# One decoder layer on one core: where the first tokens' block sums are made, how the FFN's buffers are laid out, and when the second tokens' row work is issued

## Chip, core and metric

The kernel runs on one core of a Trainium2 chip, in one launch. The metric is device microseconds of one execution, and less is better. The engines are TensorE (PE, with its weight loads as PEld), VectorE (DVE), ScalarE (ACT), GpSimd (POOL) and SyncE (SP, which here only issues DMAs). Each engine works through a queue of its own, in an order fixed when the program is built. A build-time scheduler makes that order from the program's order, priorities and its own estimate of when each instruction can start; a context `high_priority(offset=n)` moves what is inside it n places ahead (or behind, when negative).

## What is computed

One layer over 2048 tokens of width 1024, all in float32. The attention part (sliding window, state-space and compressed/selected attention) ends in a mixing product, and the FFN follows:

```
x = x + einsum('ble,ed->bld', mixed, w_out)      # mixed: three normed mixer outputs, 1024 wide
h2 = rms_norm(x, norm2_g)
hid = relu(einsum('blf,...', h2, w_up))          # 1024 -> 4096
x = x + einsum('blf,fd->bld', hid * hid, w_down) # 4096 -> 1024
```

## The kernel before

**Products.** A float32 operand is split into a rounded high part and the rest (`split`: a cast on ACT, a subtraction on DVE), and each product is three matmuls. In the FFN each 2 x 2 block product is made of seven products instead of eight, over sums and differences of blocks. The seven are named by digits and always run in the order `ORDER = "1675243"`. Factors 1, 2 and 3 are blocks of the normed tokens themselves; 5, 7, 6 and 4 are differences of blocks.

**Attention's last stage (`phase_mix`).** It goes over 16 tiles of 128 tokens. For tile i `finish_steps` lists: load the mixer rows into the tile `mix` (tag `mix`, one buffer) and the input rows into `box["x"]` (`mx` in the trace, two buffers); turn `mix` (L1190, L1192); 48 matmuls with the 16 tiles of w_out (L77 to L79, "fillers", at low priority); add and square (L1205, L1208); and for i < 8 scale the rows (`next_rows`, L1217), turn them and scale by the gain (`next_turned`, L1225, L1228), and store both halves to `hT` in DRAM (L1229). The list of tile i - 1 is merged into the steps of tile i. Everything in it shares one PSUM bank (`pw`), and the next tile's turn starts when this tile's steps are over.

**FFN up (`phase_up`).** Two groups of 1024 tokens (p = 0, 1), each against 16 slices of w_up (f). A step (p, f) is seven products of 12 matmuls. `first()` makes the first group's seven factors at the start: it loads four blocks of `hT` into the places of factors 4 and 3 (tiles `ft`), makes the four differences with `minus` on DVE and POOL (L1347), splits each into `fh` and `fl`, and loads factors 2 and 3 again through the two buffers `f_x` (`fx`). `weights(0, 0)`, the first slice of w_up (`ur`, sums `fs`, splits `uh`, `ul`), is issued in it ahead of the splits. For the second group, `fetch(m)` loads rows (`fxr`) after every third step, `sums(m)` scales them on ACT (L1380), turns them (L1385, L1387), stores the blocks, makes four differences on POOL (L1392, tile `fxt`) and stores these to `sums` in DRAM; the whole of `sums(m)` is issued at the end of step f = 3m + 2. In the last step of p = 0 the second group's factors are loaded and split one by one (`fetch_factor`, `refill`), each after the product that last used its place.

**FFN down (`phase_down`).** Eight slices of w_down, four token groups each, seven products of 12 matmuls. The split weights `dw` lie in one pool of seven, the 40 accumulators `acc` in two pools.

**Where things lie.** Pools are stacked from a common base, in the order in which they are opened, and a tile waits until what lay in its bytes is done with. Adding up the pool sizes gives, for the end of the attention (kilobytes of each partition, from the base): bias tables up to 22, keys and values `kAs` ... `Vs` 22 to 58, queries and small rows to 73, `th`/`tl`/`oT`/`ot` 73 to 85, four score slabs 85 to 117, `mx` and `mix` 120 to 132, `mh` and `ml` 132 to 140.2, and the 16 tiles of w_out from byte 143,584 on. In `phase_up` before, the seven factors fill 0 to 112, `f_s` 112 to 118, `f_x` 118 to 134, `f_ru` (raw w_up) 134 to 146, `f_st` 146 to 156, `f_u` (split w_up) 156 to 184 and `f_e` 184 to 204.

Of the kernel before, what the change touches and what calls it, by code (L numbers as in the profile page):

```python
# [16 lines left out]
P = 128  # L17
# [934 lines left out]
RING = 6  # L952


def phase_mix(tc, C, x, gains, B, cmp, w_out, out_norm_g, g2, pc, oa_d, ob, x1, hT, rr, rh, ss_a, ss_b, r_d, release):
    nc = tc.nc
    kcA, kcB, vc = cmp
    with ExitStack() as ctx:
# [210 lines left out]
        def finish_steps(i, oc):  # L1169
# [61 lines left out]
            def filler(n, k):  # L1231
                with tc.high_priority(offset=ENDS.get(i, -FILL)):
# [7 lines left out]
            return res + ([next_rows, lambda: next_turned(0), lambda: next_turned(1)] if i < NT // 2 else [])  # L1240

        def front(i):

# [50 lines left out]
AHEAD = 5  # L1294
LAG_SLOT = 2


def split(nc, dh, dl, src):

    nc.scalar.copy(dh, src)  # L1300
    nc.vector.tensor_tensor(dl, src, dh, op=ALU.subtract)  # L1301


def phase_up(tc, C, x1, rr, g2, hT, xs, w_up, vd):
# [7 lines left out]
    with ExitStack() as ctx:  # L1312
        def pool(name, bufs, **kw):
            return ctx.enter_context(tc.tile_pool(name=name, bufs=bufs, reuse_waits="tile", **kw))
        hp = pool("f_h", 1)
        es = pool("f_s", 3)
        xp = pool("f_x", 2)
        ru = pool("f_ru", 6)
        st = pool("f_st", 5)
        up_ = pool("f_u", 7)  # L1320
        ev = pool("f_e", 10)
        g2t = pool("f_g", 1).tile([P, NK], F32, name="f_g2")
        ps_u = pool("f_psu", 2, space=PSUM)
        hh, hl, W = {}, {}, {}

        for o in ORDER:
            for n in "hl":
                hp.tile([P, HALF, 4, P], F32R, tag=n + o, name=f"fo{n}{o}")
        own = {"1": (0, 0), "2": (0, 1), "3": (1, 1)}

        def slot(p, o):
            hh[o], hl[o] = (hp.tile([P, HALF, 4, P], F32R, tag=n + o, name=f"f{n}{p}{o}") for n in "hl")
# [6 lines left out]
        def first():  # L1339

            at = {n: hp.tile([P, HALF, 4, P], F32, tag=tag, name="ft" + n)
                  for n, tag in (("11", "h4"), ("12", "l4"), ("22", "h3"), ("21", "l3"), ("5", "h2"), ("7", "l2"), ("6", "h5"))}
            for n in ("11", "12", "22", "21"):
                nc.sync.dma_start(at[n], hT[0, int(n[1]) - 1, int(n[0]) - 1])

            def minus(eng, dst, x, y):
                eng.tensor_tensor(at[dst], at[x], at[y], op=ALU.subtract)  # L1347

            def keep(o, src):
                slot(0, o)  # L1350
                split(nc, hh[o], hl[o], src)
            W["u"] = weights(0, 0)
            minus(nc.vector, "5", "12", "11")
            minus(nc.gpsimd, "7", "22", "12")
            keep("1", at["11"])
            minus(nc.vector, "6", "22", "5")
            keep("6", at["6"])
            minus(nc.gpsimd, "21", "21", "6")
            keep("7", at["7"])
            keep("5", at["5"])  # L1360
            keep("2", loaded(hT[(0, *own["2"])], "02"))
            keep("4", at["21"])
            keep("3", loaded(hT[(0, *own["3"])], "03"))

        rows = {}

# [5 lines left out]

        def sums(m):

            xr = rows.pop(m)
            x = xp.tile([P, 4, HALF, P], F32, tag="x", name=f"fxb{m}")
            B, T = {}, {}
            for b in range(2):
                r = xr[:, b].rearrange("p k t -> p (k t)")
                nc.scalar.activation(r, r, AF.Copy, scale=rr[:, 8 + 4 * b + m:9 + 4 * b + m])  # L1380
            for n, (b, k) in enumerate(((0, 0), (1, 0), (1, 1), (0, 1))):
                B[b, k] = x[:, n]
                pt = ps_u.tile([P, HALF, P], F32, tag="d", name=f"fpt{m}{n}")
                for j in range(HALF):
                    nc.tensor.transpose(pt[:, j], xr[:, b, HALF * k + j], C["ident"])  # L1385
                for j in range(HALF):
                    nc.scalar.activation(x[:, n, j], pt[:, j], AF.Copy, scale=g2t[:, HALF * k + j:HALF * k + j + 1])  # L1387
                nc.sync.dma_start(hT[1, b, k, :, :, m], x[:, n])
            t = xp.tile([P, 4, HALF, P], F32, tag="x", name=f"fxt{m}")
            for n, (o, x_, y) in enumerate((("5", (1, 0), (0, 0)), ("6", (1, 1), "5"), ("7", (1, 1), (1, 0)), ("4", (0, 1), "6"))):  # L1390
                T[o] = t[:, n]
                nc.gpsimd.tensor_tensor(T[o], B[x_], T[y] if y in T else B[y], op=ALU.subtract)  # L1392
                nc.sync.dma_start(xs[n, :, :, m], T[o])

        def fetch_factor(o):
            rows[o] = loaded(hT[(1, *own[o])] if o in own else xs["5674".index(o)], "1" + o)

        def refill(o):

            slot(1, o)  # L1400
            split(nc, hh[o], hl[o], rows.pop(o))

        def weights(p, f):
# [98 lines left out]

        steps = [(p, f) for p in range(2) for f in range(NF)]
        with tc.high_priority(offset=UP_HOIST):
            first()
            nc.sync.dma_start(g2t, g2[0].rearrange("(k p) -> p k", p=P))
        for n, (p, f) in enumerate(steps):
            last = (p, f) == (0, NF - 1)
            if last:
                for o in ORDER[:2]:  # L1510
                    fetch_factor(o)
            for k, (o, step) in enumerate(zip(ORDER, up(p, f))):
                step()
                if last:
                    refill(o)
                    if k + 2 < 7:
                        fetch_factor(ORDER[k + 2])
            if p == 0 and f % 3 == 0 and f < 12:
                fetch(f // 3)
            if p == 0 and f % 3 == 2 and f < 12:  # L1520
                sums(f // 3)
            if n + 1 < len(steps):
                W["u"] = weights(*steps[n + 1])


def phase_down(tc, x1, w_down, vd, out):
# [4 lines left out]
    FC = 512  # L1531
    NC = DFF // FC
    N = 512
    LOW = 27
    with ExitStack() as ctx:
        def pool(name, bufs, **kw):
            return ctx.enter_context(tc.tile_pool(name=name, bufs=bufs, reuse_waits="tile", **kw))
        wp = pool("d_w", 7)
        ep = pool("d_e", 4)
        a_low = pool("d_a", 1)  # L1540
        rp = pool("d_r", 1)
        vr = pool("d_vr", 3)
        tp = pool("d_t", 3)
        vp = pool("d_v", 6)
        a_high = pool("d_b", 1)
        ps = pool("d_ps", 2, space=PSUM)
# [7 lines left out]

        def start_acc(m):
            for n in ("u", "22", "11", "21", "12"):
                pl = a_low if places.index((m, n)) < LOW else a_high
                acc[m, n] = pl.tile([P, N], F32, tag=f"acc{m}{n}", name=f"acc{m}{n}")
# [12 lines left out]
        def weights(c, res):  # L1571
# [107 lines left out]
def trunk(tc, x, norm1_g, w_in, qk_g, sinks, rel_bias, a_re, a_im, log_dt, b_re, b_im, c_re, c_im, d_skip, glu_w, glu_b,  # L1679
# [3 lines left out]
    with ExitStack() as ctx:  # L1683
# [27 lines left out]
        sums = dr.tile([4, P, HALF, 4, P], F32, name="sums")  # L1711
# [13 lines left out]
        with ExitStack() as c_g:  # L1725
# [18 lines left out]
        phase_mix(tc, C, x, gains, B, cmp, w_out, out_norm_g, norm2_g, pc, oa_d, ob, x1, hT, rr, rh_c, ss_a, ss_b, r_d, c_u.close)  # L1744
# [68 lines left out]
```

## Time and profile before

| | |
|---|---|
| median of 3 runs | 2646.47 us (2642.21 to 2647.43) |
| the profiled execution | 2648.5 us |
| its span, first to last instruction | 2646.7 us |
| PE busy in the span | 2505.8 us, 95% |
| granted TensorE clock, mean | 0.981 of 2.4 GHz |
| attention's last w_out matmul starts | 1354.2 us |
| first FFN product starts / second starts | 1370.3 / 1378.3 us |
| last product of FFN up, first of FFN down | 2024.2 / 2026.1 us |

Times in the text are microseconds from the start of the span. Engines are told by busy time; a matmul's record overlaps the next one's, so what counts on PE is the distance between starts. An idle time is put down to the release that came last.

### The profile page before, as it was taken

What the parts mean: (1) busy time and instruction counts of PE and PEld (TensorE: products, weight loads), DVE (VectorE), ACT (ScalarE), POOL (GpSimd) and SP (SyncE); (2) the same over time, 40 slices, a digit from 0 to 9 for tenths busy, and PEclk for the clock granted to TensorE, in tenths of its full rate; (3) what the DMA queues carried; (4) which work ended last, traced back from release to release, by engine and by line L of the source; (5) the groups of instructions that cost most, each with busy time, mean ns of one, the idle gap of its engine ahead of it and who ended that gap; (6) DMA issues with size and microseconds to landing.
All of it is one profiled execution on the core that took longest, in us unless ns stands there. A gap on an engine that the chain in (4) does not pass through costs nothing. (4 is left out here: it accounts for less than half of the span.)

```text
span 2646.7 us, 39486 instructions
## 1 busy us (share of the span) xinstructions
PE 2505.8 (95%) x13480; PEld 2116.4 (80%) x13480; DVE 1796.4 (68%) x3427; ACT 1315.2 (50%) x2774; POOL 1124.1 (42%) x1193
## 2 busy tenths in 40 slices
PE   8999999899889999999969999999999999999999
PEld 7998989677677777777848777778887888888887
DVE  3835764765686677778666556675555788888886
ACT  5344333765575666656535455544444443344442
POOL 2014442421233332313157666575654344454447
PEclk9999999899899999999989999999999999999999
DMA  4352333522222121101145666665555644444435
GB/s 124 81 149 74 87 77 86 151 63 55 67 87 69 61 65 47 49 27 45 44 158 174 192 191 195 206 202 155 148 151 166 213 131 135 129 127 127 128 96 195
DMA packets 388906, 312.71 MB, mean 118 GB/s; under 512 B 54998, under 2 KB 357724, under 8 KB 387040
## 3 DMA queue, kind: packets, MB, share of 16 engines
q1 hardware_dynamic: 352608, 285.01, 36.2%
q10 hardware_dynamic: 36096, 25.17, 3.0%
q8 instruction: 107, 1.75, 0.3%
q14 instruction: 95, 0.78, 0.1%
HBM read 201.06 MB, written 104.85 MB: 116 GB/s over the span
## 5 line engine op out<-in xcount | busy, mean ns | idle before, releaser
L1300 ACT CAST v<-vr 128x512 fp32r<-128x512 f32 x224 | 139.8, 624 | 307.5 <-DMA vr<-vd 147.0
L1301 DVE TENSOR_TENSOR v<-vr,v 128x512 fp32r<-128x512 f32 x224 | 232.6, 1045 | 81.2 <-ACT v L1300 81.0
L77 PE MATMUL pm<-wh,hh 128*128 128x256 f32 (+2 forms) x768 | 233.9, 305 | 5.4 <-ACT u_st L156 3.6
L78 PE MATMUL pm<-wl,hh 128*128 128x256 f32 (+2 forms) x768 | 226.9, 296 | 2.5 <-DVE wl L137 2.5
L79 PE MATMUL pm<-wh,hl 128*128 128x256 f32 (+2 forms) x768 | 227.0, 296 | 0.0
L1612 PE MATMUL pdc<-dw,v 128*128 128x512 f32 x768 | 185.2, 390 | 2.3 <-DVE acc L1633 1.9
L1612 PE MATMUL pda<-dw,v 128*128 128x512 f32 x768 | 185.0, 390 | 2.4 <-ACT dw L1300 1.4
L1612 PE MATMUL pdb<-dw,v 128*128 128x512 f32 x768 | 184.6, 389 | 0.1
L1612 PEld LDWEIGHTS pda<-dw,v 128*128 128x128 f32 x768 | 144.0, 188 | 33.3 <-ACT dw L1300 2.7
L1612 PEld LDWEIGHTS pdc<-dw,v 128*128 128x128 f32 x768 | 143.9, 188 | 33.3 <-DVE acc L1633 2.8
L1612 PEld LDWEIGHTS pdb<-dw,v 128*128 128x128 f32 x768 | 144.1, 188 | 30.3 <-issue 0.5
L1421 POOL TENSOR_TENSOR fs<-ur,ur 128x512 f32<-128x512 f32 x64 | 92.3, 1443 | 153.9 <-DMA ur<-in_w_up 138.2
L1301 DVE TENSOR_TENSOR ul<-ur,uh 128x512 fp32r<-128x512 f32 x96 | 102.7, 1072 | 78.3 <-ACT uh L1300 75.5
L1300 ACT CAST uh<-fs 128x512 fp32r<-128x512 f32 x128 | 78.6, 622 | 153.0 <-PE pub L1450 60.1
L77 PEld LDWEIGHTS pm<-wh,hh 128*128 128x128 f32 x768 | 147.9, 193 | 8.4 <-ACT u_st L156 3.8
L78 PEld LDWEIGHTS pm<-wl,hh 128*128 128x128 f32 x768 | 147.8, 193 | 6.6 <-DVE wl L137 3.2
L79 PEld LDWEIGHTS pm<-wh,hl 128*128 128x128 f32 x768 | 147.5, 192 | 0.1
L1301 DVE TENSOR_TENSOR ul<-fs,uh 128x512 fp32r<-128x512 f32 x128 | 137.0, 1073 | 13.9 <-ACT uh L1300 13.6
L1450 PE MATMUL pua<-fh,uh 128*128 128x512 f32 x256 | 103.7, 405 | 24.9 <-ACT uh L1300 15.7
L1466 POOL TENSOR_TENSOR ev<-e,e 128x512 f32<-128x512 f32 x64 | 100.8, 1574 | 33.7 <-ACT e L1463 33.7
L77 PE MATMUL pw<-wo_h,mh 128*128 128x512 f32 x256 | 109.3, 427 | 4.4 <-ACT mh L1192 2.8
L845 DVE TENSOR_TENSOR tls<-pps,ths 128x512 fp32r<-128x512 f32 (+1 forms) x144 | 92.7, 657 | 28.5 <-ACT ths L844 21.8
(535 smaller groups left out, 7574.8 us busy)
## 6 DMA issues: line engine op xcount, KB each, us to landing
vr<-vd SPq DMA_DIRECT2D x224, 256.0 KB
ur<-in_w_up SPq DMA_DIRECT2D x128, 256.0 KB
vd<-ev SPq DMA_DIRECT2D x128, 256.0 KB
vd<-e ACTq DMA_DIRECT2D x64, 256.0 KB
dr<-in_w_down SPq DMA_DIRECT2D x32, 512.0 KB
wr<-in_w_in SPq DMA_DIRECT2D x40, 256.0 KB
x<-in_x SPq DMA_DIRECT2D x16, 512.0 KB
mx<-in_x SPq DMA_DIRECT2D x16, 512.0 KB
```

Source lines behind the costliest of these rows:

```text
L77: nc.tensor.matmul(out, sh, mh, start=first, stop=False)
L78: nc.tensor.matmul(out, sh, ml, start=False, stop=False)
L79: nc.tensor.matmul(out, sl, mh, start=False, stop=last)
L845: nc.vector.tensor_tensor(tl[:, 0:nb], pt[:, 0:nb], th[:, 0:nb], op=ALU.subtract)
L1300: nc.scalar.copy(dh, src)
L1301: nc.vector.tensor_tensor(dl, src, dh, op=ALU.subtract)
L1421: nc.gpsimd.tensor_tensor(t, x, y, op=op)
L1450: nc.tensor.matmul(bank[b], w[:, k], h[o][:, k], start=first and k == 0 and n == 0, stop=k == HALF - 1 and n == 2, skip_group_check=True)
L1466: nc.gpsimd.tensor_tensor(tile_("v" + o), x, y, op=op)
L1612: nc.tensor.matmul(bank[b, q], x[:, q, j], y[:, j], start=first and j == 0 and n == 0, stop=j == 1 and n == 2, skip_group_check=True)
```

## The change

- In tiles 4 to 7 of the attention, a new step `partner`, put after three fillers, loads the two stored half rows of tile i - 4 into a tile of tag `mix`; a new last step `next_sums` makes the four differences on POOL and stores them to `xs`, which gets a second copy for the first group. The first half of these tiles is no longer stored to `hT`, as nothing reads it.
- `first()` is gone. All seven factors of the first group come through `f_x` with `fetch_factor` and `refill`, as the second group's do.
- The pools of `phase_up` and `phase_down` get another order. `g2t` is padded to 224 bytes (`PAD`).
- `sums(m)` becomes a list of seven pieces, issued between the products of steps f = 3m + 1 and 3m + 2. The block (1, 0) is no longer stored.

```diff
-                nc.sync.dma_start(hT[0, i // 4, half, :, :, i % 4], hx[:, 4 * half:4 * half + 4])
+                if i < 4 or half:
+                    nc.sync.dma_start(hT[0, i // 4, half, :, :, i % 4], hx[:, 4 * half:4 * half + 4])
+            def partner():
+                old = box["old"] = fp.tile([P, 2, 4, P], F32, tag="mix", name=f"mixs{i}", bufs=1)
+                for half in range(2):
+                    nc.sync.dma_start(old[:, half], hT[0, 0, half, :, :, i - 4])
+            def next_sums():
+                old, hx = box["old"], box["x"].rearrange("p (b k t) -> p b k t", b=2, t=P)
+                for o, dst, a, b in (("5", old[:, 0], hx[:, 0], old[:, 0]), ("7", hx[:, 0], hx[:, 1], hx[:, 0]),
+                                     ("6", hx[:, 1], hx[:, 1], old[:, 0]), ("4", old[:, 1], old[:, 1], hx[:, 1])):
+                    nc.gpsimd.tensor_tensor(dst, a, b, op=ALU.subtract)
+                    nc.sync.dma_start(xs[0, "5674".index(o), :, :, i - 4], dst)
...
+            if NT // 4 <= i < NT // 2:
+                res.insert(6, partner)
+                res.append(next_sums)
...
-        hp = pool("f_h", 1)
-        es = pool("f_s", 3)
-        xp = pool("f_x", 2)
-        ru = pool("f_ru", 6)
-        st = pool("f_st", 5)
-        up_ = pool("f_u", 7)
-        ev = pool("f_e", 10)
-        g2t = pool("f_g", 1).tile([P, NK], F32, name="f_g2")
+        factors(ORDER[:1])
+        st = pool("f_st", 5)
+        xp = pool("f_x", 2)
+        ru = pool("f_ru", 6)
+        up_ = pool("f_u", 7)
+        factors(ORDER[1:3])
+        ev = pool("f_e", 10)
+        es = pool("f_s", 3)
+        g2t = pool("f_g", 1).tile([P, PAD], F32, name="f_g2")
+        factors(ORDER[3:])
...
+            return [lambda b=b: scaled(b) for b in range(2)] + [
+                lambda n=n, b=b, k=k: turned(n, b, k) for n, (b, k) in enumerate(((0, 0), (1, 0), (1, 1), (0, 1)))] + [summed]
...
         with tc.high_priority(offset=UP_HOIST):
-            first()
-            nc.sync.dma_start(g2t, g2[0].rearrange("(k p) -> p k", p=P))
+            for o in ORDER[:2]:
+                fetch_factor(0, o)
+            for k, o in enumerate(ORDER):
+                refill(0, o)
+                if k == 0:
+                    W["u"] = weights(0, 0)
+                if k + 2 < 7:
+                    fetch_factor(0, ORDER[k + 2])
...
+            if p == 0 and f % 3 == 1 and f < 12:
+                parts = dict(zip(((1, 1), (1, 3), (1, 5), (2, 0), (2, 2), (2, 4), (2, 6)), sums(f // 3)))
...
-            if p == 0 and f % 3 == 2 and f < 12:
-                sums(f // 3)
...
-        wp = pool("d_w", 7)
-        ep = pool("d_e", 4)
-        a_low = pool("d_a", 1)
+        w_low = pool("d_w", 2)
+        tp = pool("d_t", 3)
         rp = pool("d_r", 1)
         vr = pool("d_vr", 3)
-        tp = pool("d_t", 3)
         vp = pool("d_v", 6)
-        a_high = pool("d_b", 1)
+        ep = pool("d_e", 4)
+        w_high = pool("d_w2", 5)
+        ap = pool("d_a", 1)
...
+        for m, n in places[-LATE:] + places[:-LATE]:
+            ap.tile([P, N], F32, tag=f"acc{m}{n}", name=f"acc{m}{n}")
...
-                t = wp.tile([P, 2, 2, N], F32R, tag="w", name=f"dw{c}{o}")
+                t = (w_low if o in ORDER[:2] else w_high).tile([P, 2, 2, N], F32R, tag="w", name=f"dw{c}{o}")
```

## Rows read from the trace of the kernel before

**Rows 1.** Stretches: length, engines' busy us (instructions), granted clock, DMA share, GB/s.
```profile
1335.20:1354.60 19.40, 14.93 (x59) 10.79 (x57) 9.53 (x6) 4.25 (x8) 12.55 (x21) 0.91 0.60 244
1354.60:1381.80 27.20, 8.84 (x25) 5.93 (x25) 21.57 (x13) 12.73 (x16) 17.46 (x14) 0.62 0.41 135
1381.80:1640.00 258.20, 249.31 (x1109) 203.76 (x1109) 157.44 (x168) 136.73 (x261) 175.54 (x115) 0.99 0.63 184
1742.00:2000.00 258.00, 258.00 (x1140) 213.70 (x1139) 146.46 (x176) 122.91 (x203) 152.84 (x108) 1.00 0.53 155
1700.00:1742.00 42.00, 31.27 (x111) 23.45 (x110) 29.99 (x25) 22.61 (x29) 22.41 (x12) 0.88 0.77 247
2020.00:2060.00 40.00, 35.72 (x151) 27.29 (x150) 30.11 (x34) 20.45 (x32) 15.25 (x9) 1.00 0.76 249
```

**Rows 2.** The chain that ended last: start, us, twelve matmuls of one product.
```profile
1741.73 2.72 PE pud L1450 x12
```

**Rows 3.** Timeline of PE: start, us, instruction, idle before it and releaser.
```profile
1354.22 0.39 PE L79 MATMUL pw<-wo_h,ml 128*128 128x512 f32 x1
1370.33 0.80 PE L1450 MATMUL pua<-fh,uh 128*128 128x512 f32 x1 [15.72 <-ACT uh L1300]
1378.31 0.50 PE L1450 MATMUL pud<-fh,uh 128*128 128x512 f32 x1 [0.91 <-ACT uh L1300]
```

**Rows 4.** Timeline of SP's queue at the end of the attention.
```profile
1338.45 2.00 SPq L1344 DMA_DIRECT2D ft<-hT  x4
1354.89 2.18 SPq L1409 DMA_DIRECT2D ur<-in_w_up  x4
```

**Rows 5.** Timeline of ACT there.
```profile
1354.43 1.90 ACT L1300 CAST fh<-ft 128x2048 fp32r<-128x2048 f32 x1 [6.83 <-POOL ft L1347]
```

**Rows 6.** Instructions of line 1347 (differences in `first`): ns min/median/max, first, last.
```profile
L1347 POOL TENSOR_TENSOR ft<-ft,ft x2: 4520/5308/6096, 1348.3 to 1359.0; 128x2048 f32<-128x2048 f32 x2
```

**Rows 7.** Timeline of DVE: the last read of the bias table.
```profile
1317.95 0.75 DVE L823 CUSTOM_DVE_ANT_0 slw<-pqw,b_sel,mx 128x512 f32<-128x512 f32 x1 [1.51 <-PE pqw L821]
```

**Rows 8.** Waits of PE, 1385 to 1640: us in total, times, longest.
```profile
PE pua L1450 <- ACT e L1470: 7.4, 3, 2.7
PE fpt L1385 <- ACT fxb L1387: 1.5, 3, 0.7
```

**Rows 9.** Timeline of ACT around 1460.
```profile
1460.75 2.42 ACT L1380 ACTIVATE fxr<-fxr,rr 128x1024 f32<-128x1024 f32 x2 [6.90 <-issue]
```

**Rows 10.** Timeline of SP's queue just ahead of that.
```profile
1450.49 4.32 SPq L1393 DMA_DIRECT2D sums<-fxt  x4
1454.98 1.61 SPq L1371 DMA_DIRECT2D fxr<-x  x2
```

**Rows 11.** Stretches in attention: tiles 4 and 7 without fillers; tiles 8 to 12.
```profile
928.70:939.80 11.10, 8.22 (x62) 7.01 (x61) 7.00 (x17) 7.44 (x21) 4.18 (x11) 1.00 0.20 71
1055.50:1066.80 11.30, 9.49 (x67) 7.99 (x67) 8.49 (x28) 9.01 (x23) 4.93 (x13) 1.00 0.23 83
1066.80:1298.00 231.20, 221.67 (x1398) 184.51 (x1397) 179.50 (x501) 137.59 (x283) 54.08 (x127) 1.00 0.10 34
```

**Rows 12.** Instructions of line 1392, differences on POOL of 128 x 512.
```profile
L1392 POOL TENSOR_TENSOR fxt<-fxb x8: 1288/1515/1745, 1448.0 to 1638.9; 128x512 f32<-128x512 f32 x8
```

**Rows 13.** SP's queue: a load of `mix` in the attention.
```profile
903.99 0.38 SPq L1176 DMA_DIRECT2D mix<-oa_d  x1
```

**Rows 14.** POOL: the last scaling of that `mix`.
```profile
908.97 0.69 POOL L1181 TENSOR_SCALAR mix<-mix,r_b 128x512 f32<-128x512 f32 x1
```

**Rows 15.** ACT: the next tile's turned rows are read.
```profile
939.84 0.59 ACT L1192 CAST mh<-ptx 128x512 fp32r<-128x512 f32 x1
```

**Rows 16.** Instructions on `slw`, 780 to 1090: DVE reads one operand from PSUM.
```profile
L823 DVE CUSTOM_DVE_ANT_0 slw<-pqw,b_sel,mx x31: 731/748/751, 780.4 to 1084.1; 128x512 f32<-128x512 f32 x31
```

**Rows 17.** Instructions on `ul`, 1381 to 1700: DVE reads both operands from SBUF.
```profile
L1301 DVE TENSOR_TENSOR ul<-fs,uh x66: 678/1172/1803, 1379.5 to 1699.2; 128x512 fp32r<-128x512 f32 x66
```

**Rows 18.** POOL at the end of FFN up: the last sum of products.
```profile
2042.60 1.72 POOL L1466 TENSOR_TENSOR ev<-e,ev 128x512 f32<-128x512 f32 x1
```

More of the change, by code (lines that the diff above doesn't have):

```diff
@@ L952, with phase_mix @@
 RING = 6
-def phase_mix(tc, C, x, gains, B, cmp, w_out, out_norm_g, g2, pc, oa_d, ob, x1, hT, rr, rh, ss_a, ss_b, r_d, release):
+def phase_mix(tc, C, x, gains, B, cmp, w_out, out_norm_g, g2, pc, oa_d, ob, x1, hT, xs, rr, rh, ss_a, ss_b, r_d, release):
     nc = tc.nc
@@ L1295 @@
 LAG_SLOT = 2
+PAD = 56
 def split(nc, dh, dl, src):
@@ L1314, in pool, with factors @@
             return ctx.enter_context(tc.tile_pool(name=name, bufs=bufs, reuse_waits="tile", **kw))
-        hp = pool("f_h", 1)
-        es = pool("f_s", 3)
+        hp = {}
+        def factors(os):
+            p = pool("f_h" + os, 1)
+            for o in os:
+                hp[o] = p
+                for n in "hl":
+                    p.tile([P, HALF, 4, P], F32R, tag=n + o, name=f"fo{n}{o}")
+        factors(ORDER[:1])
+        st = pool("f_st", 5)
         xp = pool("f_x", 2)
         ru = pool("f_ru", 6)
-        st = pool("f_st", 5)
         up_ = pool("f_u", 7)
+        factors(ORDER[1:3])
         ev = pool("f_e", 10)
-        g2t = pool("f_g", 1).tile([P, NK], F32, name="f_g2")
+        es = pool("f_s", 3)
+        g2t = pool("f_g", 1).tile([P, PAD], F32, name="f_g2")
+        factors(ORDER[3:])
         ps_u = pool("f_psu", 2, space=PSUM)
         hh, hl, W = {}, {}, {}
-        for o in ORDER:
-            for n in "hl":
-                hp.tile([P, HALF, 4, P], F32R, tag=n + o, name=f"fo{n}{o}")
         own = {"1": (0, 0), "2": (0, 1), "3": (1, 1)}
         def slot(p, o):
-            hh[o], hl[o] = (hp.tile([P, HALF, 4, P], F32R, tag=n + o, name=f"f{n}{p}{o}") for n in "hl")
+            hh[o], hl[o] = (hp[o].tile([P, HALF, 4, P], F32R, tag=n + o, name=f"f{n}{p}{o}") for n in "hl")
         def loaded(src, name):
@@ L1337, in loaded @@
             return t
[L1339 to L1363, printed above, removed]
         rows = {}
@@ L1373, in sums, with scaled, turned @@
         def sums(m):
[L1375 to L1379, printed above, removed]
+            B, box = {}, {}
+            def scaled(b):
+                r = rows[m][:, b].rearrange("p k t -> p (k t)")
                 nc.scalar.activation(r, r, AF.Copy, scale=rr[:, 8 + 4 * b + m:9 + 4 * b + m])
-            for n, (b, k) in enumerate(((0, 0), (1, 0), (1, 1), (0, 1))):
-                B[b, k] = x[:, n]
+            def turned(n, b, k):
+                if n == 0:
+                    box["x"] = xp.tile([P, 4, HALF, P], F32, tag="x", name=f"fxb{m}")
+                B[b, k] = box["x"][:, n]
@@ L1383, in sums @@
                 pt = ps_u.tile([P, HALF, P], F32, tag="d", name=f"fpt{m}{n}")
                 for j in range(HALF):
-                    nc.tensor.transpose(pt[:, j], xr[:, b, HALF * k + j], C["ident"])
+                    nc.tensor.transpose(pt[:, j], rows[m][:, b, HALF * k + j], C["ident"])
                 for j in range(HALF):
-                    nc.scalar.activation(x[:, n, j], pt[:, j], AF.Copy, scale=g2t[:, HALF * k + j:HALF * k + j + 1])
-                nc.sync.dma_start(hT[1, b, k, :, :, m], x[:, n])
@@ L1389, in sums @@
[L1389 to L1396, printed above, removed]
@@ L1398, in refill, with summed @@
-        def refill(o):
-            slot(1, o)
+                    nc.scalar.activation(B[b, k][:, j], pt[:, j], AF.Copy, scale=g2t[:, HALF * k + j:HALF * k + j + 1])
+                if (b, k) != (1, 0):
+                    nc.sync.dma_start(hT[1, b, k, :, :, m], B[b, k])
+            def summed():
+                rows.pop(m)
+                t = xp.tile([P, 4, HALF, P], F32, tag="x", name=f"fxt{m}")
+                T = {}
+                for n, (o, x_, y) in enumerate((("5", (1, 0), (0, 0)), ("6", (1, 1), "5"), ("7", (1, 1), (1, 0)), ("4", (0, 1), "6"))):
+                    T[o] = t[:, n]
+                    nc.gpsimd.tensor_tensor(T[o], B[x_], T[y] if y in T else B[y], op=ALU.subtract)
+                    nc.sync.dma_start(xs[1, n, :, :, m], T[o])
@@ L1401, in refill, with fetch_factor @@
+            return [lambda b=b: scaled(b) for b in range(2)] + [
+                lambda n=n, b=b, k=k: turned(n, b, k) for n, (b, k) in enumerate(((0, 0), (1, 0), (1, 1), (0, 1)))] + [summed]
+        def fetch_factor(p, o):
+            rows[o] = xp.tile([P, HALF, 4, P], F32, tag="x", name=f"fx{p}{o}")
+            nc.sync.dma_start(rows[o], hT[(p, *own[o])] if o in own else xs[p, "5674".index(o)])
+        def refill(p, o):
+            slot(p, o)
             split(nc, hh[o], hl[o], rows.pop(o))
@@ L1510, in phase_up @@
                 for o in ORDER[:2]:
-                    fetch_factor(o)
+                    fetch_factor(1, o)
+            if n == 0:
+                nc.sync.dma_start(g2t[:, 0:NK], g2[0].rearrange("(k p) -> p k", p=P))
+            if p == 0 and f % 3 == 1 and f < 12:
+                parts = dict(zip(((1, 1), (1, 3), (1, 5), (2, 0), (2, 2), (2, 4), (2, 6)), sums(f // 3)))
             for k, (o, step) in enumerate(zip(ORDER, up(p, f))):
                 step()
+                if p == 0 and (f % 3, k) in parts:
+                    parts.pop((f % 3, k))()
                 if last:
-                    refill(o)
+                    refill(1, o)
                     if k + 2 < 7:
-                        fetch_factor(ORDER[k + 2])
+                        fetch_factor(1, ORDER[k + 2])
             if p == 0 and f % 3 == 0 and f < 12:
                 fetch(f // 3)
-            if p == 0 and f % 3 == 2 and f < 12:
-                sums(f // 3)
             if n + 1 < len(steps):
@@ L1533, in phase_down @@
     N = 512
-    LOW = 27
+    LATE = 9
     with ExitStack() as ctx:
@@ L1556, in start_acc @@
             for n in ("u", "22", "11", "21", "12"):
-                pl = a_low if places.index((m, n)) < LOW else a_high
-                acc[m, n] = pl.tile([P, N], F32, tag=f"acc{m}{n}", name=f"acc{m}{n}")
+                acc[m, n] = ap.tile([P, N], F32, tag=f"acc{m}{n}", name=f"acc{m}{n}")
                 if n != "u":
@@ L1710, in trunk @@
         hT = dr.tile([2, 2, 2, P, HALF, 4, P], F32, name="hT")
-        sums = dr.tile([4, P, HALF, 4, P], F32, name="sums")
+        sums = dr.tile([2, 4, P, HALF, 4, P], F32, name="sums")
         dkp = dr.tile([G, 16, 368], F32, name="dkp")
@@ L1743, in trunk @@
             run(merge(swa, glu, b_nsa + c_steps))
-        phase_mix(tc, C, x, gains, B, cmp, w_out, out_norm_g, norm2_g, pc, oa_d, ob, x1, hT, rr, rh_c, ss_a, ss_b, r_d, c_u.close)
+        phase_mix(tc, C, x, gains, B, cmp, w_out, out_norm_g, norm2_g, pc, oa_d, ob, x1, hT, sums, rr, rh_c, ss_a, ss_b, r_d, c_u.close)
         c_b.close()
```

5 lines of the change are left out of this document (4 added, 1 removed).

## The prediction

> **What bounds the kernel now.** I read the stretches first, then PE's timeline at the places where PE is not full, then the waits there, and last the queues of the engine that PE waited for. From 1742 to 2000 PE is busy all of the 258.0 us [rows 1], and twelve matmuls of one product take 2.72 us [rows 2], 0.2267 us each. FFN up and down hold 2 x 2688 such matmuls, so only PE's gaps can be won there. They lie in four places:
>
> - The start of FFN up. Attention's last w_out matmul starts at 1354.22; the first product waits 15.72 us for ACT, to 1370.33, and the second starts at 1378.31 [rows 3]. The 27.2 us to 1381.8, where the third begins, hold the 24 matmuls of two products, 5.4 us: 21.8 us are lost. The granted clock in them is 0.62 [rows 1]: PE had stood still, and the first product's matmuls run partly at 1.2 GHz.
> - The second tokens' row work, 1381.8 to 1640: PE is idle 258.2 - 249.3 = 8.9 us, and a mean clock of 0.99 [rows 1] costs up to 2.6 more: 11.5 us.
> - The refill of the factors, 1700 to 1742: 42 us hold 185 matmuls at the full rate, 111 are recorded [rows 1], so about 74 x 0.2267 = 16.8 us.
> - The start of FFN down, 2020 to 2060: 176 against 151 [rows 1], 5.7 us.
>
> Why the first is so long: SP starts the loads of `ft` only at 1338.45 and the first slice of w_up at 1354.89 [rows 4], because their places lie under buffers that the attention used to the end (`ft` under `oT`/`ot`, `ur` under `mh`, `ml` and w_out). Then ACT's casts stand behind `first`'s chain of differences, as at 1354.43, where it waited 6.83 us for POOL [rows 5]; one difference takes POOL 4.5 to 6.1 us [rows 6]. The reader is to see a chain of loads, differences and splits that begins where attention ends.
>
> **The change, part by part.** *Start of FFN up.* By the new order of pools, factor 1 lies at 0 to 16 KB, over the bias table last read at 1317.95 [rows 7]; `f_x` over keys; raw w_up over keys, queries and the first of the values; the split w_up over small rows of the attention; factors 6 and 7 over the score slabs and `oT`/`ot`; factors 5, 2, 4 and 3 exactly over w_out tiles 0 to 7, which come free one after the other up to 1354.2. So from about 1320 on, loads of 1 MB, casts of 1.90 us [rows 5] and subtractions that take somewhat longer can go ahead under the last w_out products. The four differences are ready in DRAM. With two buffers and some 10 us for load, cast and subtraction, I work out (an estimate) factor 1 split at 1324, 7 at 1334, 6 at 1343 (it waits for `ot`), 5 at 1349, 2 at 1353, 4 at 1358, 3 at 1363. PE needs the fourth at 1354.4 + 3 x 2.72 = 1362.6 and the seventh at 1370.7. All are in time, so the whole 21.8 us go; I take 22. Two small things I let cancel: casts and subtractions of some 2 us now stand in the queues of ACT and DVE among attention's last steps (0 to 4 us lost), and PE's 19.4 - 14.9 = 4.5 idle us from 1335 on [rows 1], with the slow clock behind them, can now be filled with the first products (0 to 5 us won). Bounds: if the supply is as bad as in the refill, which takes the same way through two buffers, 17 us remain lost and only 5 are won; at best 27.
>
> *Second tokens' row work.* PE waits three times, 7.4 us together, for the copy of product 1 on ACT, and 1.5 us for the turned rows [rows 8]. Ahead of one of the three, ACT had stood 6.90 us at the row scaling of 1460.75 [rows 9], because SP issued that fetch only at 1454.98, behind stores of differences that took from 1450.49 on [rows 10] as POOL had not made them yet. Nothing is removed here, the same 2 scalings, 16 turns and 4 differences are issued, but the pieces end about one step (19 us) earlier, so the differences are over when the next fetch comes, and ACT's 16 small scalings stand four at a time between products. I take 9 of the 11.5 us (the three waits and the slow clock behind them); bounds 0, if ACT stands at a late fetch all the same, and 11.5.
>
> *Differences in the attention.* Four tiles get two loads, four subtractions and four stores each, and lose one store: 16 subtractions of 1.29 to 1.75 us [rows 12], 23 us of POOL, which is busy less than half of the time. SP issues 20 transfers more, at about half a microsecond 10 us of a queue that mostly waits. What costs is the wait: `mix` has one buffer. Before, the load of the next `mix` starts at 903.99 [rows 13] and the tile is ready at 909.7 [rows 14], 30 us before it is turned at 939.84 [rows 15]. Now the old rows sit in that place until the last store of a difference has landed. From the last scaled half row, just ahead of that turn, it is about 4.5 us for the three subtractions left, 2.5 us for the store (an estimate from the 2 us or so that SP stands at L1179 between a store to `hT` and the next load), and the same 5.7 us from load to ready: 12 us later than before, four times. Behind it stand the next tile's turn and all its fillers, so for 48 us PE has only the attention's own matmuls. What PE does then is in the trace: in the four stretches of tiles 4 to 7 without fillers (45.9 us, of which the first and last are shown) it is idle 7.9 us, 17%, and from 1066.8 to 1298, with fillers at hand, 9.5 of 231.2 us, 4% [rows 11]. 48 x 0.13 = 6.3; I take 7 us lost. The fillers themselves are made up for in tiles 8 to 12, whose windows are twice as long as 48 matmuls need. Bounds: 0 if the scheduler hides the wait, 14 if the idle share doubles.
>
> A rule of the Trainium skill speaks against this part. What rows show: a DVE subtraction with both operands in SBUF takes 0.68 us at best and 1.17 at the median, 1.80 at worst [rows 17], where POOL works beside it; the attention's own DVE work, one operand of which is in PSUM, stays at 0.73 to 0.75 us [rows 16]. The skill's GPSIMD Engine Reference, section Key points, says that POOL shares its SBUF interfaces with VectorE and contends with instructions that read two SBUF operands. By that rule taken for all of DVE the 23 us of POOL would stretch DVE's work in the attention and the sum would lose some 11 us more; by the rows it costs nothing there, and I go by the rows.
>
> *FFN down.* The weights' places come free earlier for factors 6 and 7 and later for 5, which now lies on four `f_e` buffers that POOL may read until its last sum, 2042.60 + 1.72 in the trace [rows 18], while PE would want that weight at about 2034. The scheduler can put ACT's squares of the last product ahead, and then POOL is done near 2035. From 5 us won to 10 lost; I take 0. The refill at 1700 is not changed by any edit: its 16.8 us stay.
>
> **The sum.** The profiled execution takes 2648.5 us, 1.8 more than its span: 2648.5 - 22 - 9 + 7 = 2624.5. The median of the runs lies 2.0 below that execution: 2622.5 us. By 0.2% (5 us), about what a measurement of this kernel can tell from no change, this is clearly faster.
>
> **The rivals.** (a) *Supply-bound start*: loads through two buffers feed the seven factors no faster than at 1700, and 17 us of the 22 stay. For it: the same path and sizes. Against it: some 30 us of lead in which the places are free. 2646.5 - 5 - 9 + 7 = 2639.5. (b) *The other side: the `mix` wait holds the attention up.* SP's queue is in order, so the loads of the attention's own tiles (`tc`) stand behind the late `mix` load too; if its main chain then stops with the fillers, PE stands in the 4 x 12 us, not for 17% but for nearly all of them: + 40 instead of + 7, 2646.5 - 31 + 40 = 2655.5. It decides from 31 us on, that is from 65% idle in these stretches. Against it: even without fillers PE was 83% busy. (c) *POOL against DVE*, the rule above: 2622.5 + 11 = 2633.5. (d) *The early splits don't come early*: the scheduler puts them behind attention's work in the queues, or SP's first load stands in front of a late place, and the start stays as it was: 2646.5 - 9 + 7 = 2644.5. (e) *More is won*: the tail is filled with products, and the wait for `mix` is hidden: 2646.5 - 27 - 11 = 2608.5, and 3 for FFN down.
>
> **Chances.** Forecast 0.55, with a range of its own of 2613 to 2632; (a) 0.15; (b) 0.08; (c) 0.04; (d) 0.06; (e) 0.12. From (e) at 2605 to (d) at 2645, 8 in 10 and a little more are inside. Faster by over 0.2% (below 2641.2): forecast, (a) for the most part, (c), (e): 0.86; within 0.2%: (d) and a little of (a): 0.06; slower: (b): 0.08.
>
> **What would show it.** Right: the first `fh` cast near 1320 and the first FFN product no later than a few microseconds after the last w_out matmul, at the full clock; no wait of over 2 us of product 1 for ACT between 1381 and 1640; `mix` loads of tiles 5 to 8 that start some 12 us later against the turn before them, and PE idle about 7 us more from 900 to 1300; the refill's gap as before. Wrong: seven products at the start that each wait for `fl`; an attention that ends over 15 us later; a new gap at the fourth product of FFN down.

## The result and the profile after

The changed kernel takes 2687.7 us (median of 4 runs, 2678.1 to 2688.4) against 2646.6: a ratio of 1.0147, 95% interval 1.0124 to 1.0171. It is 41 us slower, where 24 us faster were forecast. The profiled execution has a span of 2686.0 us, against 2646.7.

Both spans can be cut at the same events: the copy `mh` that follows the turn of a tile (L1192), the last w_out matmul, and the steps of 84 matmuls of FFN up and down. "Bare" is an undisturbed step (the mean of steps 20 to 30, 19.04 before and 19.39 after). A step's start is the start of its first matmul.

| stretch | before | after | difference |
|---|---|---|---|
| start to the turn of tile 0 (no edit there) | 727.0 | 731.7 | +4.7 |
| turn of tile 0 to turn of tile 9 | 379.4 | 420.3 | +40.9 |
| turn of tile 9 to turn of tile 15 | 232.4 | 232.7 | +0.3 |
| turn of tile 15 to the last w_out matmul | 15.3 | 29.6 | +14.3 |
| from there to the end of step 0, over a bare step | 22.2 | 3.5 | -18.7 |
| steps 1 to 12 (row work), over the bare steps | 21.6 | 6.8 | -14.8 |
| steps 13 to 19 (refill), over the bare steps | 17.2 | 15.2 | -1.9 |
| 31 bare steps of FFN up, 19.04 and 19.39 each | 590.2 | 601.0 | +10.8 |
| last step and the first five of FFN down, over the bare steps | 8.2 | 11.7 | +3.6 |

The sum is 39.2, the spans differ by 39.3; the rest of FFN down takes the same time in both. The first line is no effect: in the 17 traces of this study tile 0 is turned anywhere from 723.0 to 733.2, with no edit to the work ahead of it. One trace against another can be some 10 us off by that alone.

Stretches of the trace after, columns as in [rows 1]. First tiles 4 to 8; then the four without fillers, which answer to [rows 11]; then the end of the attention and the row work:

```profile
906.10:1119.20 213.10, 179.10 (x1022) 146.96 (x1021) 131.77 (x392) 109.64 (x269) 73.72 (x132) 0.92 0.23 71
931.80:962.10 30.30, 21.13 (x134) 17.85 (x132) 14.95 (x39) 15.52 (x38) 15.59 (x30) 0.83 0.28 92
984.80:1013.50 28.70, 21.47 (x127) 17.31 (x128) 17.98 (x52) 16.46 (x40) 14.63 (x28) 0.88 0.34 106
1036.10:1064.50 28.40, 21.08 (x126) 17.43 (x126) 19.01 (x58) 16.39 (x41) 16.88 (x31) 0.88 0.33 107
1091.80:1119.20 27.40, 20.71 (x139) 16.63 (x138) 19.53 (x57) 16.38 (x40) 15.96 (x30) 1.00 0.35 112
1384.60:1414.40 29.80, 16.04 (x52) 12.21 (x53) 13.41 (x12) 12.13 (x15) 13.76 (x20) 0.71 0.30 106
1440.00:1700.00 260.00, 260.00 (x1162) 212.25 (x1162) 157.58 (x171) 141.89 (x269) 176.57 (x120) 1.00 0.67 194
```

The four stretches sum to 114.8 us where they were 45.9: 17 us longer each. PE is idle 30.4 us in them (7.9 before), and the granted clock, 1.00 before, is 0.83 to 0.88 in three of them. In the last row, the row work, PE is busy all the time.

Why a tile's turn is late shows on the queues at tile 4. The waits of ACT between 906.1 and 1119.2 (total, times, longest), and the timelines of SP, POOL, ACT and PE:

```profile
ACT mix L874 <- DMA sums<-mixs: 11.2, 4, 4.2
```
```profile
942.62 0.58 SPq L1230 DMA_DIRECT2D hT<-mx  x1
943.68 5.38 SPq L1243 DMA_DIRECT2D sums<-mx  x2
949.89 0.52 SPq L1243 DMA_DIRECT2D sums<-mixs  x1
...
952.53 0.33 SPq L1176 DMA_DIRECT2D mix<-oa_d  x1
```
```profile
947.24 1.28 POOL L1242 TENSOR_TENSOR mx<-mx,mixs 128x512 f32<-128x512 f32 x1 [3.59 <-DMA hT<-mx]
```
```profile
952.58 0.42 ACT L874 ACTIVATE mix<-oc 128x256 f32<-128x256 f32 x1 [4.22 <-DMA sums<-mixs]
```
```profile
953.62 0.79 PE L849 MATMUL pow<-thw,vw 128*128 128x256 f32 x2 [4.22 <-ACT thw L844]
```

POOL's third difference overwrites rows whose store to `hT` has not landed, and waits 3.59 us. The last store of a difference goes out at 949.89. ACT's next instruction is the square for the norm of tile 5 (L874), which uses the last quarter of `mix` as scratch: ACT stands 4.22 us until that store has landed, and PE stands behind it for a cast of the main chain.

The end of the attention, on PE and on DVE:

```profile
1393.32 0.40 PE L78 MATMUL pw<-wo_l,mh 128*128 128x512 f32 x1
1404.34 0.80 PE L77 MATMUL pw<-wo_h,mh 128*128 128x512 f32 x1 [10.62 <-DVE ml L1193]
1404.93 0.63 PE L78 MATMUL pw<-wo_l,mh 128*128 128x512 f32 x1
1405.36 0.63 PE L79 MATMUL pw<-wo_h,ml 128*128 128x512 f32 x1
...
1414.21 0.40 PE L79 MATMUL pw<-wo_h,ml 128*128 128x512 f32 x1
1414.44 0.39 PE L1461 MATMUL pua<-fh,uh 128*128 128x512 f32 x1
```
```profile
1391.78 0.69 DVE L1322 TENSOR_TENSOR ul<-ur,uh 128x512 fp32r<-128x512 f32 x1 [5.85 <-POOL mix L876]
1392.39 2.96 DVE L1322 TENSOR_TENSOR ul<-fs,uh 128x512 fp32r<-128x512 f32 x3
1395.27 3.41 DVE L1322 TENSOR_TENSOR ul<-ur,uh 128x512 fp32r<-128x512 f32 x2
1398.60 0.68 DVE L1322 TENSOR_TENSOR ul<-fs,uh 128x512 fp32r<-128x512 f32 x1
1399.20 4.48 DVE L1322 TENSOR_TENSOR fl<-fx,fh 128x2048 fp32r<-128x2048 f32 x2
1403.60 0.68 DVE L1193 TENSOR_TENSOR ml<-ptx,mh 128x512 fp32r<-128x512 f32 x1
```

The FFN's splits now do go ahead (the first `fh` cast starts at 1368.4), and the first product starts 0.23 us behind the last w_out matmul. But seven `ul` and two `fl` stand ahead of the second half of tile 15's `ml`, and PE stands 10.62 us for it. Then its starts lie 0.43 us apart, the lower clock, until 1409. Part of the delay is a place: DVE stands 5.85 us ahead of the first `ul` for POOL's last read of `oc` (L876), the rows that the norm of tile 15 scales. In the built program this `ul` shares 32 bytes with tile 15's `oc`. Without that stand the nine splits could have ended some 6 us earlier (an estimate from this row; not tried).

The chain that ended last, after, one step of products in the order 1675243 (against [rows 2]):

```profile
1808.27 2.75 PE pua L1461 x12
1811.01 2.72 PE pud L1461 x12
1813.73 2.72 PE puc L1461 x12
1816.45 2.80 PE pub L1461 x12
1819.25 2.80 PE pua L1461 x12
1822.05 2.80 PE puc L1461 x12
1824.85 2.80 PE pub L1461 x12
```

Products 5, 2, 4 and 3 take 2.80 us at a granted clock of 1.00 and without a wait, in every step.

### The profile page after: what moved, and what is told of

Its sections match the earlier page's. It is cut to its first block, busy times and chain, and to the rows that moved or that the text cites. A ratio compares the mean times of both kernels' runs of the same rounds, so it can differ in the third digit from the quotient of the medians.

```text
span 2686.0 us, 39538 instructions
## 1 busy us (share of the span) xinstructions
PE 2534.6 (94%) x13480; PEld 2133.0 (79%) x13480; DVE 1792.0 (67%) x3425; ACT 1319.6 (49%) x2774; POOL 1129.6 (42%) x1207
## 5 line engine op out<-in xcount | busy, mean ns | idle before, releaser
L1322 DVE TENSOR_TENSOR v<-vr,v 128x512 fp32r<-128x512 f32 x224 | 238.0, 1070 | 78.6 <-ACT v L1321 78.5
L1322 DVE TENSOR_TENSOR ul<-fs,uh 128x512 fp32r<-128x512 f32 x128 | 135.1, 1059 | 20.1 <-ACT uh L1321 19.9
L77 PE MATMUL pw<-wo_h,mh 128*128 128x512 f32 x256 | 110.6, 432 | 16.8 <-DVE ml L1193 10.8
L78 PE MATMUL pw<-wo_l,mh 128*128 128x512 f32 x256 | 106.6, 416 | 1.2 <-DVE wo_l L1025 1.1
```

What stands on the lines that cost most here:

```text
L77: nc.tensor.matmul(out, sh, mh, start=first, stop=False)
L78: nc.tensor.matmul(out, sh, ml, start=False, stop=False)
```

## The experiments

Ratios are against the kernel before, which ran beside them (medians of 2645.8 to 2647.5 us). Diffs are against the changed kernel unless said otherwise.

**No differences in the attention.**

```diff
-            if NT // 4 <= i < NT // 2:
-                res.insert(6, partner)
-                res.append(next_sums)
```

> The changed kernel without its new steps in tiles 4 to 7: no old rows loaded, no differences, none stored (factors 5, 7, 6 and 4 of the first group are read from stored blocks instead, so the output is not the layer's; loads, splits and products of FFN up keep their number and size). Theory A (the +41 us that lie between the turns of tiles 4 and 9 in the trace after come from these steps): 2687.7 - 41 = 2647, tile 9 turned near 1111, and the wait at the end of the attention stays. Theory B (they cost the 7 us of the prediction, and the rest of the attention's delay comes from loads and splits of the FFN that were pulled ahead): 2680 or more.

2642.8 us, ratio 0.9981 (0.9968 to 0.9993): 45 us less. Tile 9 is turned at 1107.9, and PE's wait for `ml` is still there. Theory A; the prediction's 7 us for this part falls.

**The old rows in another place.**

```diff
-                old = box["old"] = fp.tile([P, 2, 4, P], F32, tag="mix", name=f"mixs{i}", bufs=1)
+                old = box["old"] = fp.tile([P, 2, 4, P], F32, tag="xt", name=f"mixs{i}", bufs=2)
...
+            if NT // 4 < i <= NT // 2:
+                res.insert(3, load_x)
```

In these tiles `load_x` has the two lines for `box["x"]` that stood in `load`.

> The changed kernel with the old rows in a tile of tag xt (two buffers, shared with the input rows) and not of tag mix; in tiles 5 to 8 the input rows are loaded after the turn. All differences, loads and stores are made. Theory A1 (the cost lies in the one place of mix: ACT's square of the next tile's normed part writes there and stands until the last store has landed, 4.2 us in the first of four tiles, and the engines behind it with it): ACT's wait for the stores is gone, 36 to 41 us come back, 2647 to 2652. Theory A2 (the 16 subtractions on POOL and the 20 transfers on SP cost it, wherever the rows lie): 2675 or more. Between them, each has a share.

2647.7 us, 0.9999 (0.9989 to 1.0010): 40 us less, with every difference, load and store made. Tiles 4 to 8, before and in its trace:

```profile
901.70:1066.80 165.10, 152.94 (x953) 126.74 (x950) 121.00 (x370) 103.34 (x255) 52.51 (x116) 1.00 0.17 55
898.60:1068.10 169.50, 155.10 (x954) 127.40 (x953) 122.75 (x369) 103.79 (x256) 69.89 (x129) 1.00 0.24 77
```

169.5 us, against 165.1 before and 213.1 after, at the full clock. So the place costs 40 (the later load of the input rows goes with it and was not tried alone), and the work itself some 5 (against the kernel without differences).

**ACT's stand alone.**

```diff
+            late["sq"] = wp.tile([P, 256], F32, name="wo_sq")
-        nc.scalar.activation(dst, flat, AF.Square, accum_out=ss)
+        nc.scalar.activation(dst if scratch is None else scratch, flat, AF.Square, accum_out=ss)
...
-                A.normed(mix[:, 768:D], oc, f"c{i}")
+                A.normed(mix[:, 768:D], oc, f"c{i}", late["sq"])
```

> The changed kernel with the square of the normed part written to a place of its own (1 KB of each partition) and not into mix, so that ACT has nothing to wait for there; mix itself is held by the old rows as long as before. Theory G (ACT's stand, with PE behind it and then at the lower clock, is most of the 41 us): 20 us or more back, 2668 or less. Theory H (the late turn of mix is most of it, as nothing but the attention's own matmuls is at hand): 2680 or more.

2677.8 us, 1.0111 (1.0095 to 1.0126): 10 us less, between the two theories. Tiles 4 to 8 in its trace:

```profile
909.90:1109.20 199.30, 172.42 (x1022) 140.10 (x1019) 132.22 (x392) 109.66 (x268) 73.77 (x132) 0.97 0.24 76
```

ACT no longer waits for a store, and 14 of the 48 us come back in these tiles. `mix` is late all the same, and PE waits for POOL's scaling of it at each of the four turns, 6.4 us together. So about a quarter of the 40 us is ACT's stand. The other 30, the difference to the run before this one, come with `mix` being held, that is with the late turns; how they divide further was not tried.

**32 bytes of padding.**

```diff
-PAD = 56
+PAD = 64
```

> The changed kernel with PAD = 64 for 56: factors 5, 2, 4 and 3 of FFN up lie 32 bytes higher, nothing else moves. In the trace after twelve matmuls of products 5, 2, 4 and 3 take 2.80 us where products 6 and 7 take 2.72, in all 32 steps: 11.0 us in all. Theory C (it is the start address of these factors, which differs by 32 from a multiple of 64 against the others): all products at 2.72 us, 2687.7 - 11 = 2677. Theory D (these products are slowed by something else, such as the upper part of the memory or work beside them): 2.80 us stay, 2687 to 2689.

2677.0 us, 1.0111 (1.0094 to 1.0128): 10.7 less, all products at 2.72. Theory C, for the products. That the whole time fits as well is partly luck: the bare steps win 10.8 in the trace, but steps 1 to 12 (9.0 over bare steps, for 6.8), the refill (17.1 for 15.2) and the start of FFN down (13.7 for 11.7) lose about 6 of it again. In its trace the rest of the difference lies ahead of FFN up, where the padding changes nothing.

**Where the weights lie.**

```diff
-PAD = 56
+PAD = 48
+        pool("f_p", 1).tile([P, 8], F32, name="f_pad")
         up_ = pool("f_u", 7)
```

> The changed kernel with 32 bytes between f_ru and f_u and PAD = 48: the split slices of w_up (the weights that PE loads) and factors 6 and 7 move up by 32 bytes to multiples of 64; factors 5, 2, 4 and 3 stay at multiples of 64; factor 1 stays 32 bytes off. Theory C1 (a product is slow where the start addresses of weights and moving operand differ by 32 from one another): only product 1 at 2.80 us, 2687.7 - 11 + 2.6 = 2679. Theory C2 (a product is slow where the moving operand starts at a multiple of 64): products 6, 7, 5, 2, 4 and 3 at 2.80, 2687.7 + 5 = 2693. Theory C3 (the moving operands' place in the upper part of the memory): as after, 2688.

2687.0 us, 1.0150 (1.0134 to 1.0166). One step of its chain, in the same order of products:

```profile
1810.19 2.80 PE pua L1462 x12
1812.99 2.75 PE pud L1462 x12
1815.73 2.72 PE puc L1462 x12
1818.45 2.80 PE pub L1462 x12
1821.25 2.80 PE pua L1462 x12
1824.05 2.80 PE puc L1462 x12
1826.85 2.80 PE pub L1462 x12
```

Products 1, 5, 2, 4 and 3 are slow and 7 is fast (6 begins behind a slow one). None of the three theories says this.

**Agreement modulo 128.** 24 floats of padding ahead of `f_u`, 8 behind it, PAD = 24.

> The changed kernel with 96 bytes ahead of f_u, 32 behind it and PAD = 24: factors 5, 2, 4 and 3 lie where they lie in the changed kernel, the split slices of w_up are moved so that their start agrees with these four modulo 128 bytes, and factors 1, 6 and 7 no longer agree with them. If a product is slow where the starts of weights and moving operand differ modulo 128: products 5, 2, 4 and 3 at 2.72 us, 1, 6 and 7 at 2.80. If the moving operand's own place decides: 5, 2, 4 and 3 stay at 2.80.

2684.3 us (one run), all seven products at 2.78 to 2.81. The first reading falls with 5, 2, 4 and 3. The second has these four right, but product 1 is now slow too, and its factor has not moved.

**Agreement modulo 256.** PAD = 96, and PAD = 128.

> The changed kernel with PAD = 96: factors 5, 2, 4 and 3 start 128 bytes higher than with PAD = 64, where all products took 2.72 us. In the five layouts so far a product was fast where the starts of its weights and of its factor agreed modulo 256 bytes, and slow in every other case. Theory C5 (modulo 256): products 5, 2, 4 and 3 at 2.80 us again. Theory C6 (it is enough that the start is 32 off a multiple of 64, as with PAD = 64): all at 2.72.

> The changed kernel with PAD = 128: factors 5, 2, 4 and 3 start 256 bytes higher than with PAD = 64, so that they agree with the weights modulo 256 but not modulo 512 at one and the same time. Theory C5 (modulo 256): all products at 2.72 us. If only the one place of PAD = 64 was fast: 2.80.

With 96, products 5, 2, 4 and 3 at 2.79 to 2.80; with 128, all at 2.72. Of the readings tried, only agreement modulo 256 is left (table in the last section). The whole times, 2676.5 and 2679.6 us (one run each), do not show the pace: with 128 the products win 10.1 us in the trace, and steps 1 to 12, the refill and the start of FFN down lose 9.8.

**Tile 15's turns first.**

```diff
+            def turned_(h):
+                with tc.high_priority(offset=3000) if i == NT - 1 else nullcontext():
+                    turned(h)
...
-[lambda h=h: turned(h) for h in range(2)]
+[lambda h=h: turned_(h) for h in range(2)]
```

> The changed kernel with the two turns of tile 15 at a priority above the FFN's first splits, so that DVE makes ml of tile 15 ahead of six of the seven ul and of two fl. Theory E (in the trace after PE stands 10.6 us for ml behind these splits, and then runs at the lower clock): 11 to 14 us come back, 2674 to 2677, with the first product of FFN up still right behind the last one of attention. Theory F (the splits are then late for FFN up, which waits as long): 2684 or more.

2673.7 us, 1.0094 (1.0076 to 1.0112): 14 less by the medians. In the trace the stretch from the turn of tile 15 to the last w_out matmul falls from 29.6 to 20.2, and the start of FFN up stays (3.5 and 3.8 us over a bare step). Theory E. Of the 20.2, 6.1 is a wait for tile 15's norm on POOL, which the wait for `ml` had covered in part.

**The row work in one block.** `sums(m)` whole behind the last product of step f = 3m + 2; and, the other way round, the seven pieces alone in the kernel before.

> The changed kernel with the second tokens' row work issued in one block after the last product of steps f = 3m + 2, as before the change. The steps of FFN up in the two traces say that the pieces won 14.7 us there (21.6 us over the bare products before, 6.9 of them the turns themselves; 6.9 after): 2687.7 + 14.7 = 2702. If the gain came from the new places of the buffers and not from the pieces: 2688 to 2691. The prediction's figure of 9: 2697.

> The kernel before with one part of the change alone: the second tokens' row work in seven pieces (the block (1, 0) is still stored). If the pieces cure the three waits for ACT in these steps, as the prediction has it: 9 to 15 us faster, 2632 to 2638. If the waits come from POOL's lateness since the start of FFN up (raw w_up landed late, so that the differences end 6 us later against the steps than in the changed kernel with one block): less than 5 us, 2642 to 2647, and steps 1 to 12 keep most of their 21.6 us over the bare products.

The block: 2685.1 us, 1.0147 (1.0131 to 1.0164), as after. The pieces in the kernel before: 2644.5, 0.9987 (0.9978 to 0.9996). Steps 1 to 12 over the bare steps, of which 6.8 are the turns, tell the parts apart, by one trace each:

| | one block | seven pieces |
|---|---|---|
| FFN up as before | 21.6 | 15.2 |
| FFN up as after | 12.3 | 6.8 |

In these steps the pieces win about 6 us, and the rest of the new FFN up (its start, its places, one store less) about 9. My 14.7 for the pieces was wrong. In the whole time the pieces win less: 3 us in the kernel before, and nothing that the runs can tell in the changed kernel (2685.1 without them, 2687.7 with them). That is what the rival readings said: less than 5 us, with most of the 21.6 left (15.2). In the changed kernel with one block ACT stands at the row scaling for 3.94 us, against 6.90 in [rows 9]:

```profile
1489.40 2.41 ACT L1380 ACTIVATE fxr<-fxr,rr 128x1024 f32<-128x1024 f32 x2 [3.94 <-DMA fxr<-x]
```

**The pools of FFN down as before.**

> The changed kernel with the pools of FFN down as before the change. If the new order of these pools costs the 3.5 us that the first steps of FFN down are longer: from the last product of FFN up to the fifth step of FFN down some 3 to 4 us less than in the trace after. If the start of FFN down hangs on something else: as after.

2694.8 us (one run). PE's waits at the start of FFN down:

```profile
PE pda L1634 <- ACT dw L1321: 20.6, 1, 20.6
```

The theory falls: under the new FFN up the old order of pools is 15 us worse in this stretch, 26.3 over the bare steps instead of 11.7.

**The three repairs together:** the other place, PAD = 64, tile 15's turns first.

> The changed kernel with the three repairs together: old rows in tag xt, PAD = 64, tile 15's turns at a high priority. If the three causes are separate and add up: 2687.7 - 40 - 11 - 14 = 2623, which is 24 us faster than before. If they share idle time (an attention that ends earlier only waits longer for the FFN's factors): 2632 or more.

2636.2 us, 0.9955 (0.9942 to 0.9968): 51.5 of the 65 us. With bare steps of 19.04 again, steps 1 to 12 lose 11.0 instead of 6.8 and steps 13 to 19 lose 17.7 instead of 15.2. So part of the shortfall is shared time, as the second reading has it: the engines that feed PE had gained time from its slower products. In all five traces of the new FFN up with every product at 2.72, steps 1 to 12 lose 9.0 to 11.3 us; in those with slow products, without the block, 6.8 to 8.5.

**And tile 15's load at the high priority;** then its norm's eight small steps on DVE as well.

> The kernel with the three repairs, and the load and norm of tile 15 at the high priority as well as its turns. In the trace with the three repairs PE stands 6.1 us for the norm of tile 15's mix on POOL, behind the FFN's sums of w_up and the row norm of tile 14. If the priority brings the norm ahead of them: 3 to 5 us less than with the three repairs, 2632. If POOL's order stays as it is there: 2635 to 2637.

> The kernel with the three repairs and tile 15's load at the high priority, and the eight small steps of tile 15's norm made on DVE and not on POOL. In the trace with the three repairs PE stands 6.1 us for this norm, which POOL makes behind the row norm of tile 14 and a sum of w_up. If POOL's queue is the cause: 3 to 5 us less than the 2634 to 2636 of the kernels with three repairs, 2631. If DVE's queue is as long: 2634 to 2636.

The priority alone: 2633.9, 0.9955 (0.9941 to 0.9970); POOL's order of the norm stays, and so does the wait of 6.1 us. With the norm on DVE: 2629.9 us (2627.4 to 2631.6), 0.9931 (0.9918 to 0.9945), 16 us faster than before and the best kernel here. The turn of tile 15 is 15.2 us from the last w_out matmul, as before the change, and PE's wait for the norm is 1.8:

```profile
PE ptx L1194 <- POOL mix L876: 1.8, 1, 1.8
PE pua L1470 <- DVE fl L1331: 1.3, 1, 1.3
PE ptx L1194 <- POOL fs L1441: 1.2, 1, 1.2
```

## Why the prediction was wrong, step by step

- *Start of FFN up, -22:* -18.7, the first product right behind the last w_out matmul at the full clock, as forecast. That the casts and subtractions "cancel" against products in the tail failed: the queue of DVE cost 14.3 us, where 0 to 4 were allowed. The step looked at how long such an instruction is, and not at how many the scheduler would put ahead of one `ml`, nor at what the first of them waits for.
- *Row work, -9 (bound 11.5):* -14.8. The bound was too low: before, steps 1 to 12 stood 21.6 - 6.8 = 14.8 us over bare steps and turns. The mechanism held for about 6 in these steps, and for 3 in the whole time of the kernel before. Some 9 come with the rest of the new FFN up, so that the size of the gain is partly luck. How stays open: with one block the last row difference ends 6.8 us ahead of step 4 (1483.0, 1489.8) and before it ended 1.0 us ahead (1453.6, 1454.6), but POOL's waits for raw w_up are no shorter there (24.7 us from 1410 to 1495, against 19.9 from 1380 to 1460).
- *Differences in the attention, +7 (bounds 0 to 14):* +40.9. This is the step that failed. It let the next turn come 12 us late; it comes 17 late, in part because the third difference waits for a store too. It named POOL, SP and the next turn as what waits, but `mix` is also written by ACT, whose queue carries the main chain (about 10 of the 40 us). And it priced the late turn by PE's idle share alone, 17% as before; it was 26%: of the 48 us by which tiles 4 to 8 are longer, 21.8 are idle (34.0 against 12.2, from the rows of tiles 4 to 8 above). Some 11 are 69 more matmuls (an estimate, at the mean of 0.16 us of the stretch before); tile 8's stretch is 6.8 shorter for it. The rest, some 15, goes with the lower clock behind PE's stands (0.92 in the mean, against 1.00). From tile 9 on nothing is made up (232.4 and 232.7).
- *FFN down, 0; refill unchanged:* +3.6 and -1.9. The first product of FFN down waits 3.1 us for ACT's `v`, which the step did not weigh.
- *Not in the sum:* 10.8 us of slower products, of which some 5 or less are left in the whole time (an estimate from the traces with PAD = 64 and 128, where 6 and 10 of it come back as waits).
- *The rivals:* (b) came true in size (+40), but not as it was told: SP stood at the loads of `mix` for 4.0 us in all, and PE was idle for 26% of these stretches, not for 65%. (a) and (d) fell with the start of FFN up, (e) with the wait for `mix`. (c) did not come: DVE's busy time in tiles 4 to 8 is 122.75 us for 369 instructions with all differences made and the old rows elsewhere, and 121.00 for 370 before. The Trainium skill's GPSIMD Engine Reference, Key points, names DVE instructions with two SBUF inputs among those that contend with POOL; these rows agree, as far as the attention's own are like those of [rows 16], with one operand in PSUM.
- With the three harms taken out the change gives 2636.2, 14 us from the forecast and outside its range of 2613 to 2632. Only with tile 15's load and norm moved too, which the forecast's kernel does not do, it gives 2629.9, inside the range.

## What to carry to other kernels

A place that is shared is held by everything that writes it, scratch outputs included: list each engine that touches it, and ask what else stands in that engine's queue. Work that is pulled ahead is free only where nothing of the critical chain is issued behind it on the same engine; look for the last small instruction of the old stage. After a new layout of buffers compare the duration of the same product before and after, at the full clock and without waits: a shift of 32 bytes cost 10.8 us of product time here, though part of it would have been waits otherwise.

## What the runs showed of the hardware

The pace of FFN up's matmuls depends on the start addresses of its two SBUF operands. The starts are those of the built programs, modulo 256 bytes:

| layout | weights | factor | twelve matmuls |
|---|---|---|---|
| before; PAD 64; PAD 128 | 96 | 96 | 2.72 us |
| after: 1, 6, 7 | 96 | 96 | 2.72 |
| after: 5, 2, 4, 3 | 96 | 64 | 2.80 |
| weights + 32: 7 (6 follows a slow one: 2.75) | 128 | 128 | 2.72 |
| weights + 32: 1 | 128 | 96 | 2.80 |
| weights + 32: 5, 2, 4, 3 | 128 | 64 | 2.80 |
| weights + 96: 1 | 192 | 96 | 2.80 to 2.81 |
| weights + 96: 6, 7 | 192 | 224 | 2.80 |
| weights + 96: 5, 2, 4, 3 | 192 | 64 | 2.78 to 2.80 |
| PAD 96: 5, 2, 4, 3 | 96 | 224 | 2.79 to 2.80 |

Fast means equal, in all seven layouts; each difference tried (32, 64, 96 and 128 bytes) costs about the same 3%. A fast product behind a slow one takes a value between (2.73 to 2.75). The w_out products of the attention have weights and moving operand both at 64, and at the end of the trace after they are fast too: from 1411.03 to 1414.21 fourteen starts lie 0.227 us apart. Among the attention's other matmuls their starts are too uneven to tell. Why was not tried, nor whether operands of other shapes behave so.

Behind a stand of PE of 4.22 us in the attention the granted clock was 0.50 to 0.51 from 953.6 to 962.1, that is 1.2 GHz. Behind one of 10.62 us ten starts lay 0.43 us apart, the same lower level. Here such a stand cost more than its length.
